# Gram, R and attention value products over the whole TensorE array: keys and queries beside zeros, values stored twice

## The chip, the core and the metric

The kernel runs on one core of a Trainium2 chip. TensorE (PE) multiplies, VectorE (DVE), ScalarE (ACT) and GpSimd (POOL) do the elementwise work, and nearly all transfers are issued from SyncE's queue (SP). The metric is the device time in microseconds (us); less is better. Three runs of the kernel before took 4266.24, 4277.43 and 4285.46 us; the median is 4277.43 us.

## The reference

Two layers of an encoder are applied to a sequence of 2048 tokens and one of 512, with 1024 channels, in float32. Layer 0 is a pair of gated linear recurrences. Layer 1 (where the change lies) is window attention and RWKV-7 time mixing side by side, then an output product, residual and layer norm. What matters of layer 1:

```python
def banded_window_attention(q, k, v, sink):     # 8 heads of 64, 2 groups of keys and values, 128 keys either way
    s = jnp.einsum('bnigrd,bnjgd->bngrij', qb, kb).astype(jnp.float32) * (hd ** -0.5)
    ...
    p = jnp.exp(s - lse[..., None])
    o = jnp.einsum('bngrij,bnjgd->bnigrd', p.astype(vb.dtype), vb)

def rwkv7_scan(r, log_w, k, v, kk, a):          # 8 heads of 64, both directions
    def step(S, inp):
        r_t, w_t, k_t, v_t, kk_t, b_t = inp
        s_kk = jnp.einsum('bhvk,bhk->bhv', S, kk_t)
        S = S * w_t[:, :, None, :] - s_kk[..., None] * b_t[:, :, None, :] + v_t[..., None] * k_t[:, :, None, :]
        return S, jnp.einsum('bhvk,bhk->bhv', S, r_t)
```

## The kernel before

Tokens come in 5 blocks of 512. Layer 0 and the projections of both layers come first; the change lies behind them, in `layer1_core`, and in the two things that feed it: the scratch `z_scr` that `rwkv_dirs` writes, and `rwkv_post`.

`layer1_core` works on 20 steps (4 pairs of heads by 5 blocks), each in two directions and two halves of 4 chunks of 64 tokens: 80 halves. For a half, `stageA` loads `Z` (the tile `Zc`: scaled keys and queries of two heads, one on partitions 0 to 63, the other on 64 to 127) and makes on TensorE: the **Gram products** (`gram`, 2 heads by 4 chunks, each over the 64 partitions of its head); the transposed keys (`bk`, 4 transpositions); the **R products** (`rps`, per chunk one product for each head with 64 columns of weights from `LR`, and with the head's tile `SW` of 128 columns as the moving operand, where 64 rows of `SW` are an identity and 64 are values). `inverse` inverts 16 by 16 triangles on DVE, `stageT` widens the inverses with many small products (`px`, `py`, 32 by 32), multiplies them with R (`t`), overwrites the identity rows of `SW` with the result, makes `fin`, and then writes the identity back into `SW` for the next half that uses it (`unit_rows`, on POOL). `chain` carries the state from chunk to chunk: a product, two DVE additions, a transposition, an ACT copy.

`attend` is the window attention, 40 tiles of 128 queries: four heads' `score` products, the softmax on DVE and ACT, then per head the transposed probabilities (`pt<-pr`) and the **value products** (`po<-pT,vw`, 64 columns of weights, 128 moving columns, up to 3 key tiles). It holds one of two PSUM tiles of its pool for `po` during all four heads.

A lane of generators for each of these is advanced in turn; the build's scheduler then orders the instructions of each engine by its own estimates, with `stageT`, `chain` and `inverse` given priority. The engines take their instructions in that order. `rwkv_post` (head norm and gate of a block) runs for the first block beside the end of the core, in four buffers of its own; the output product `out_proj` follows it.

A product of float32 operands shows as two MATMUL records with a weight load (LDWEIGHTS) each: 640 Gram products are 1280 records. In a row, `64*128` is the part of the array that the weights take (rows and columns), and the shape behind it is the moving operand.

Of the kernel before, what the change touches and what calls it, by code (L numbers as in the profile page):

```python
# [10 lines left out]
F32 = mybir.dt.float32  # L11
# [10 lines left out]
NB = 512  # L22
# [18 lines left out]
class Common:  # L41
# [86 lines left out]
    def split(self, x, hi, lo, eng=None):  # L128
        """x into two float32r parts"""
# [4 lines left out]
    def mm2(self, out, lhsT, x):  # L134
        """product of a matrix that float32r holds exactly with two parts"""
# [7 lines left out]
    def ln_exp(self):  # L143
        """the table set of ScalarE that has both the logarithm and the exponential"""
        self.tc.keep_in_program_order(self.nc.scalar.preload_act_table_set("natural_log_exp_and_others"))

# [16 lines left out]
    # ---- products of column tiles with a block of tokens; a block comes in parts of some k-tiles, and the parts  # L163
    # stream through the buffers (one more than the parts) of one tag: [128, k-tiles, (hi, lo), tokens] ----
    def stream(self, order, load, parts):
        """order: the blocks in turn; load(i, f): part f of entry i"""
# [16 lines left out]
    def projs(self, ws, last=False):  # L183
        """one or two column tiles, part by part; last: the last of this block"""
# [17 lines left out]
    def mod_init(self):  # L202
# [9 lines left out]
        # sums the rows 32 j + s of each sequence s  # L212
# [7 lines left out]
    def mod_tiles(self, l, w, t0, nt):  # L220
        """nt column tiles of the modulation product from loaded weights w [128, 8, nt * 128]: the conditioning
        vectors stand in four column groups, each summing two of the k-tiles; the groups are added in the transposition"""
# [21 lines left out]
    def mod_first(self):  # L244
        """shift and scale of layer 0"""
# [10 lines left out]
    def mod_rest(self):  # L256
        """gate of layer 0 and all of layer 1, beside the projections"""
# [12 lines left out]
    def gate_rows(self, l, pool):  # L270
        """1 + gate over the free axis, the same on every partition"""
# [96 lines left out]
class Even(Common):  # L368
# [9 lines left out]
    def even_layer(self, mk_emit):  # L378
# [4 lines left out]
        with ExitStack() as ctx:  # L383
# [6 lines left out]
            self.wk = self.pool(ctx, "wk")  # L390
            self.sm = self.pool(ctx, "sm", 2)
# [19 lines left out]
    def even_consts(self):  # L411
# [11 lines left out]
        # lower bounds: softmax over the two logits, first entry  # L423
# [7 lines left out]
        # f = lb + oml * sigmoid(z) = (lb + oml / 2) + oml / 2 * tanh(z / 2); the halves of q and 1 - f go with nol  # L431
# [8 lines left out]
        # low-rank gate weights of GLA, stacked [hi; hi; lo]  # L440
# [36 lines left out]
    def seq_sums(self, s, n):  # L477
        """sums over the chunks of a sequence, with room for a shift by one either way: the sums of chunk c stand at
        c + 2 (forward) or c (backward), and the states before it at c + 1, where those of the chunk it follows stood"""
# [5 lines left out]
    def decay(self, lf, rows, rev, b, bc, cols, nch0):  # L485
        """rows: partitions. b: running sums in each chunk, bc: the same less its middle; cols: middle, end less middle."""
# [15 lines left out]
    def silu_from(self, ps, out, tag="sg"):  # L502
        """twice the SiLU: (1 + tanh(x / 2)) x"""
# [4 lines left out]
    def att(self, kf, qf, kb, qb):  # L508
        """masked chunk products of both directions, summed: [128 j, 4, 128 i]"""
# [35 lines left out]
    def post(self, o, col, b):  # L545
        """head RMS norm, gate, and the two float32r parts to scratch"""
# [21 lines left out]
    def out_split(self, y, col, b, pool=None):  # L568
        nc = self.nc
        yh, yl = (pool.tile([128, NB], F32R, tag=x, bufs=1 + (pool is not self.wk), name=x) if pool else self.wt(x, dt=F32R) for x in ("yh", "yl"))  # L570
# [1177 lines left out]
```

## Time and profile before

| | us |
|---|---|
| median of three runs | 4277.43 |
| span of the profiled execution | 4263.0 |
| PE busy in the span | 3864.8 (91%) |
| DVE, ACT, POOL busy | 2844.7, 2178.4, 1257.9 |
| stretch of `stageA`, 2640 to 3806 us: PE busy | 1131.58 of 1166 |
| the same stretch: DVE, ACT, POOL busy | 817.79, 680.03, 323.64 |

The profiled execution's own time is its span and some 14 us around it, taking the median of the runs for it (4277.43 - 4263.0). A matmul is busy in the record from its start to its last result, and matmuls overlap, so PE's busy share is near 100% wherever it always has work; what a group costs PE is read from the starts of the groups around it in the timeline. The granted clock (PEclk) is 1.00 where TensorE has its 2.4 GHz, and 0.50 where it has 1.2 GHz.

### The profile page before, as it was taken

The page shows a single profiled execution, that of the slowest core. Times are in us where ns is not written, and L with a number is a line of the kernel's source. Part 1 is how long each engine was busy: PE and PEld are TensorE (multiplying, and loading weights), DVE is VectorE, ACT ScalarE, POOL GpSimd, SP SyncE. Part 2 cuts the span into 40 slices and gives each one's busy share as a digit, 9 for nine tenths or more (in the row PEclk, how much of TensorE's full clock was granted, in tenths as well). Part 3 has the DMA queues.
Part 4 walks back from the last instruction along what each step waited for, and adds up shares of the span by engine and source line. Part 5 has one row for each costly group of instructions (what it writes and reads, how often), then busy time and mean ns, then how long its engine had stood idle before and what let it go on. Part 6 is the DMA issues. An engine that isn't in the chain of part 4 may idle for free.

```text
span 4263.0 us, 76423 instructions
## 1 busy us (share of the span) xinstructions
PE 3864.8 (91%) x28536; PEld 3097.3 (73%) x28536; DVE 2844.7 (67%) x6350; ACT 2178.4 (51%) x4214; POOL 1257.9 (30%) x1561
## 2 busy tenths in 40 slices
PE   6999999998888699998999897999999999997688
PEld 4878787767676478776878676778778777775467
DVE  4554545466766589577666767677767766775798
ACT  4565757455455522345544546555556555564220
POOL 1020212112211254324232422223223222233784
PEclk8999999999999799999999998989989998996799
DMA  7544544456555477678687777344344433433675
GB/s 270 198 158 149 198 163 147 175 202 214 196 210 196 144 244 244 222 255 266 230 286 242 243 248 216 102 109 107 104 104 116 104 103 97 109 98 112 217 235 179
DMA packets 672115, 768.58 MB, mean 180 GB/s; under 512 B 243680, under 2 KB 538464, under 8 KB 646144
## 3 DMA queue, kind: packets, MB, share of 16 engines
q1 hardware_dynamic: 671744, 763.69, 55.4%
q8 instruction: 226, 3.70, 0.4%
q14 instruction: 145, 1.19, 0.1%
HBM read 533.84 MB, written 220.20 MB: 177 GB/s over the span
## 4 chain that ended last, share of the span: by engine, by line
PE 31%; DVE 11%; DMA 6%; ACT 3%; issue 2%; POOL 2%; SPq 1%; POOLq 0%; DVEq 0%; ACTq 0%
PE pp L126 10%; PE gram L126 3%; PE po L126 3%; PE rps L126 2%; PE fin L126 2%; PE chain L126 2%; PE pt L141 2%; PE t L126 2%; PE py L126 1%; PE px L126 1%; PE chain L141 1%; PE score L126 1%; DVE tmp L116 1%; PE bk L141 1%; DVE Z L116 1%
## 5 line engine op out<-in xcount | busy, mean ns | idle before, releaser
L126 PE MATMUL pp<-h,whi 128*128 128x512 f32 (+2 forms) x4800 | 1560.1, 403 | 83.7 <-DMA h<-h_scr 25.4
L126 PEld LDWEIGHTS pp<-h,whi 128*128 128x128 f32 (+2 forms) x4800 | 892.1, 190 | 294.5 <-DMA h<-h_scr 25.6
L126 PE MATMUL pp<-h,wlo 128*128 128x512 f32 (+2 forms) x2400 | 955.4, 399 | 5.0 <-POOL wlo L113 5.0
L126 PEld LDWEIGHTS pp<-h,wlo 128*128 128x128 f32 (+2 forms) x2400 | 454.3, 189 | 110.0 <-POOL wlo L113 7.5
L110 ACT ACT_TABLE_LOAD x227 | 291.2, 1283 | 23.1 <-DVE cl L499 10.4
L126 PE MATMUL pp<-owh,oh 128*128 128x512 f32 x640 | 258.6, 405 | 18.8 <-DMA oh<-o_scr 16.7
L126 PE MATMUL pp<-owh,ol 128*128 128x512 f32 x640 | 255.9, 401 | 15.6 <-DMA ol<-o_scr 15.6
L126 PE MATMUL pp<-owl,oh 128*128 128x512 f32 x640 | 258.2, 404 | 0.0
L113 POOL TENSOR_TENSOR wlo<-wst,whi 128x512 fp32r<-128x512 f32 (+3 forms) x87 | 162.1, 1869 | 246.7 <-ACT whi L110 244.2
L1312 POOL COPY LD<-GS 32x128 f32<-32x128 f32 x320 | 116.9, 365 | 355.5 <-ACT GS L1309 346.8
L113 POOL TENSOR_TENSOR at<-abuf,abuf 64x256 f32<-64x256 f32 x80 | 63.7, 796 | 518.7 <-DVE abuf L529 449.2
L126 PE MATMUL gram<-Zc 64*128 64x128 f32 x1280 | 202.6, 300 | 8.8 <-DMA Zc<-z_scr 7.1
L113 DVE TENSOR_TENSOR SS<-chain,OH 64x64 f32<-64x64 f32 x608 | 135.1, 222 | 109.7 <-PE chain L126 98.7
L113 POOL TENSOR_TENSOR tmp<-tmp 128x512 fp32r<-128x512 f32 x80 | 118.5, 1481 | 254.7 <-ACT tmp L110 208.4
L126 PEld LDWEIGHTS gram<-Zc 64*128 64x128 f32 x1280 | 160.9, 196 | 42.2 <-issue 18.5
L1257 POOL COPY SW<-c_ident 64x512 f32<-64x512 f32 x160 | 106.7, 668 | 271.6 <-PE fin L126 231.5
L126 PE MATMUL fin<-GB,SW 128*128 128x128 f32 x1280 | 176.4, 280 | 2.1 <-ACT OH L1424 1.9
L110 ACT ACTIVATE S<-chain,ecol 128x128 f32<-128x128 f32 x320 | 116.3, 368 | 113.5 <-PE chain L141 110.3
L113 POOL TENSOR_TENSOR ptmp<-ptmp 128x512 f32<-128x512 f32 (+1 forms) x100 | 146.0, 1473 | 84.4 <-ACT ptmp L110 39.5
L126 PEld LDWEIGHTS fin<-GB,SW 128*128 128x128 f32 x1280 | 158.6, 193 | 10.6 <-ACT OH L1424 3.6
L126 PEld LDWEIGHTS pp<-owh,oh 128*128 128x128 f32 x640 | 124.9, 195 | 48.5 <-DMA oh<-o_scr 15.0
L126 PE MATMUL chain<-RX,S 128*128 128x128 f32 x608 | 145.5, 327 | 13.6 <-DVE od L113 10.1
(324 smaller groups left out, 8418.4 us busy)
## 6 DMA issues: line engine op xcount, KB each, us to landing
h<-h_scr SPq DMA_DIRECT2D x70, 2048.0 KB, 9.4
h<-h_scr SPq DMA_DIRECT2D x80, 1024.0 KB, 7.5
z_scr<-Z SPq DMA_DIRECT2D x40, 1024.0 KB, 4.6
Zc<-z_scr SPq DMA_DIRECT2D x80, 512.0 KB, 4.0
h_scr<-h SPq DMA_DIRECT2D x10, 2048.0 KB, 7.7
oh<-o_scr SPq DMA_DIRECT2D x40, 512.0 KB, 5.7
ol<-o_scr SPq DMA_DIRECT2D x40, 512.0 KB, 6.6
h_scr<-h1s SPq DMA_DIRECT2D x20, 1024.0 KB, 5.3
```

The lines of the kernel that those rows point to most:

```text
L110: self.nc.scalar.activation(out=out, in_=in_, func=func, bias=bias, scale=scale)
L113: (eng or self.nc.vector).tensor_tensor(out=out, in0=a, in1=b, op=op)
L116: (eng or self.nc.vector).scalar_tensor_tensor(out=out, in0=a, scalar=s, in1=b, op0=op0, op1=op1)
L126: self.nc.tensor.matmul(out=out, lhsT=lhsT, rhs=rhs, start=start, stop=stop)
L141: self.nc.tensor.transpose(out, in_, self.ident[0:n, 0:n])
L1257: nc.gpsimd.tensor_copy(sw[h][Q[h]], self.ident[Q[h]].unsqueeze(1).to_broadcast([64, 4, 128]))
L1312: nc.gpsimd.tensor_copy(LD[blk, cs], gs[blk, :, 32 * i:32 * i + 32])
```

## The change

- **Gram:** `Z` keeps only the weights' half. The moving half is loaded into one of two fixed tiles `KR`, zeroed once, where each head's columns stand beside zeros in the other head's partitions. A product takes all 128 partitions.
- **R:** the two products per chunk are now one of `kr` (128 columns of weights, both heads) with a 64-column identity `II`, and one of `la` (128 columns, both heads, a single fixed tile with zeros off the diagonal) with `vs`, the values of both heads, loaded a second time. Each has 64 moving columns instead of 128. `SW` needs no identity rows any more: `unit_rows` (two POOL copies per half) and 16 ACT copies ahead of the core go; the second copy of `t` into `SW` swaps its halves.
- **Attention:** values are loaded twice side by side, so that the weights have 128 columns; the probabilities of four heads are transposed into one tile, and one product per key tile has 512 moving columns. Half of its result is used; the gate product is two DVE instructions instead of one.
- `z_scr` has another layout. `rwkv_post` beside the core takes its buffers from the pool of the attention, under the tag that the probabilities use (5 buffers for both). Comments are dropped.

```diff
@@ rwkv_consts, rwkv_dirs @@
-        self.z_scr = self.dram.tile([4, 2, nb, 128, 8, 256], F32, name="z_scr")
+        self.z_scr = self.dram.tile([4, 2, nb, 128, 2, 8, 128], F32, name="z_scr")
...
-            Z = self.wk.tile([128, 8, 256], F32, tag="Z", bufs=1, name="Z")
+            Z = self.wk.tile([128, 2, 8, 128], F32, tag="Z", bufs=1, name="Z")
@@ layer1_core @@
-            def unit_rows(sw):
-                for h in range(2):
-                    nc.gpsimd.tensor_copy(sw[h][Q[h]], self.ident[Q[h]].unsqueeze(1).to_broadcast([64, 4, 128]))
             for i in range(NS):
                 for d in range(2):
                     for h in range(2):
-                        o = Q[1 - h]
-                        (nc.vector, nc.gpsimd)[h].memset(SW[d][i][h][o, :, Q[h]], 0.0)
-                        nc.scalar.copy(SW[d][i][h][Q[h]], self.ident[Q[h]].unsqueeze(1).to_broadcast([64, 4, 128]))
+                        (nc.vector, nc.gpsimd)[h].memset(SW[d][i][h][Q[1 - h], :, Q[h]], 0.0)
+
+            KR = [zeroed(f"KR{i}", [128, 4, 2, 2, 64], nc.gpsimd) for i in range(2)]
+            la = zeroed("LA", [128, 4, 128], nc.vector)
+            II = cp.tile([128, 64], F32, name="II")
+            for h in range(2):
+                nc.vector.tensor_copy(II[Q[h]], self.ident[Q[h], Q[h]])
+            nA = [0]
...
-                        Z = lp.tile([128, 4, 256], F32, tag="Z", bufs=2, name="Zc")
-                        nc.sync.dma_start(out=Z, in_=self.z_scr[p, d, b, :, cs])
-                        nc.sync.dma_start(out=rho, in_=self.z_scr[p, d, b, :, cs, 64:128])
-                        LR = lp.tile([128, 4, 128], F32, tag="LR", bufs=2, name="LR")
+                        kr = KR[nA[0] % 2]
+                        nA[0] += 1
+                        Z = lp.tile([128, 4, 128], F32, tag="Z", bufs=2, name="Zc")
+                        nc.sync.dma_start(out=Z, in_=self.z_scr[p, d, b, :, 1, cs])
+                        for hd in range(2):
+                            nc.sync.dma_start(out=kr[Q[hd], :, :, hd],
+                                              in_=self.z_scr[p, d, b, Q[hd], 0, cs].rearrange("p c (a t) -> p c a t", t=64))
+                        nc.sync.dma_start(out=rho, in_=self.z_scr[p, d, b, :, 0, cs, 64:128])
+                        vs = lp.tile([128, 4, 64], F32, tag="vs", bufs=2, name="vs")
                         for hd in range(2):
                             o = Q[1 - hd]
-                            nc.sync.dma_start(out=LR[Q[hd], :, Q[hd]], in_=self.z_scr[p, d, b, Q[hd], cs, 0:64])
+                            nc.sync.dma_start(out=vs[o], in_=self.v_scr[p, d, b, :, cs, o])
                             nc.sync.dma_start(out=sw[hd][o, :, o], in_=self.v_scr[p, d, b, :, cs, o])
...
-                                self.mm(ps[:, c], Z[q, c, 128:256], Z[q, c, 0:128])
+                                self.mm(ps[:, c].rearrange("p (a t) -> p a t", t=64), Z[:, c], kr[:, c, :, hd])
...
-                            self.tt(LR[o, :, q], gs[o, :, 0:64], mS[o], ALU.mult)
+                            self.tt(la[o, :, q], gs[o, :, 0:64], mS[o], ALU.mult)
...
-                        rp = pr.tile([128, 4, 128], F32, tag="t", name="rps")
+
+                        rp = pr.tile([128, 4, 2, 64], F32, tag="t", name="rps")
                         for c in range(4):
-                            for hd in range(2):
-                                self.mm(rp[Q[hd], c], LR[:, c, Q[hd]], sw[hd][:, c])
-                        nc.scalar.copy(R, rp)
+                            self.mm(rp[:, c, 0], kr[:, c, 0].rearrange("p h t -> p (h t)"), II)
+                            self.mm(rp[:, c, 1], la[:, c], vs[:, c])
+                        nc.scalar.copy(R, rp.rearrange("p c a t -> p c (a t)"))
...
-                            unit_rows(sw)
...
-                        self.add("post", self.rwkv_post(i, nb_, self.wk, 4))
+                        self.add("post", self.rwkv_post(i, nb_, self.ap, 5))
@@ attend @@
-        V = ap.tile([128, 6, 64], F32, tag="vw", bufs=1, name="vw")
-        nc.sync.dma_start(out=V[:, 0:(w1 - w0) // 128], in_=self.av_scr[g, :, w0 // 128:w1 // 128])
+
+        V = ap.tile([128, 6, 128], F32, tag="vw", bufs=1, name="vw")
+        for i in range(2):
+            nc.sync.dma_start(out=V[:, 0:(w1 - w0) // 128, 64 * i:64 * i + 64],
+                              in_=self.av_scr[g, :, w0 // 128:w1 // 128])
...
-                for i in range(nt):
-                    self.mm(po[r, hd // 2], V[:, (k0 - w0) // 128 + i], pT[:, i * 128:(i + 1) * 128],
-                            start=(i == 0), stop=(i == nt - 1))
+            po = self.pa.tile([128, 2, 2, 128], F32, tag="s", name="po")
+            for i in range(nt):
+                self.mm(po.rearrange("p a b q -> p (a b q)"), V[:, (k0 - w0) // 128 + i],
+                        pT[:, i].rearrange("p h q -> p (h q)"), start=(i == 0), stop=(i == nt - 1))
```

PE's order in the middle of the core, before (`chain`, `px`, `rps`, `gram`, `po`, `pt` as above):

```order
L126 MATMUL po<-pT,vw 64x128 x3
L141 MATMUL pt<-c_ident,pr 128x128 x3
L126 MATMUL rps<-SW_21670,LR 64x128
L126 MATMUL gram<-Zc 128x128 x4
L126 MATMUL chain<-RX,S_30413 128x2x64
L126 MATMUL px<-TT,LO 32x32 x5
L126 MATMUL chain<-RX,S_30456 128x2x64
L126 MATMUL px<-TT,LO 32x32 x4
L126 MATMUL po<-pT,vw 64x128 x3
L141 MATMUL pt<-c_ident,pr 128x128 x3
```

And about as far on, after:

```order
L126 MATMUL rps<-vs,LA 128x64
L126 MATMUL chain<-RX,S_29766 128x2x64
L126 MATMUL gram<-KR_21700,Zc 128x128 x2
L126 MATMUL chain<-RX,S_29779 128x2x64
L126 MATMUL gram<-KR_21700,Zc 128x128
L126 MATMUL t_29577<-R,TL_21656 128x128
```

Of the ten groups before, each takes another part of the array than the one ahead of it; of the six after, all take the whole array, and only `px` and `py` take less.

SP's order in the same part of the core, after (`lm` and `acc_scr` belong to the inverses and the states, `q`, `gt`, `yh`, `yl` to the attention):

```order
L1300 DMA Zc<-z_scr 128x512
L1302 DMA KR_21700<-z_scr 64x8x64
L1648 DMA o_scr<-yh 128x2x128
L1602 DMA gt<-ag_scr 128x2x128
L1648 DMA o_scr<-yl 128x2x128
L1302 DMA KR_21700<-z_scr 64x8x64
L1308 DMA vs<-v_scr 64x4x64 x2
```

A half now has eight loads where it had six, and a load of `KR` waits for the R products of two halves earlier, as one of `LR` did.

The end of the core on PE, before (`dg` makes the gate rows of `out_proj`, `cmean` and `bmean` are the products of `rwkv_post`, `pp` are those of `out_proj`):

```order
L126 MATMUL pt<-ptmp,cmean 128x512
L141 MATMUL chain<-c_ident,SS_21662 128x128
L141 MATMUL chain<-c_ident,SS_21666 128x128
L126 MATMUL pt<-dg,allones 128x128 x2
L126 MATMUL pt<-ptmp,bmean 128x512
L126 MATMUL pt<-dg,allones 128x128 x2
L126 MATMUL pt<-ptmp,bmean 128x512
L126 MATMUL pt<-dg,allones 128x128 x12
L126 MATMUL pp<-owh_39959,oh 128x512
```

And after:

```order
L141 MATMUL chain<-c_ident,SS_21666 128x128
L126 MATMUL pt<-ptmp,bmean 128x512
L126 MATMUL pt<-dg,allones 128x128 x4
L126 MATMUL pt<-ptmp,bmean 128x512
L126 MATMUL pt<-dg,allones 128x128 x12
L126 MATMUL pt<-ptmp,cmean 128x512 x2
L126 MATMUL pt<-ptmp,bmean 128x512 x2
L126 MATMUL pp<-owh_39546,oh 128x512
```

Before, half of the fourth head's `rwkv_post` stands behind the last state; after, half of the third and all of the fourth.

## Rows read from the trace of the kernel before

**Rows 1.** The page's first line.

```profile
span 4263.0 us, 76423 instructions
```

**Rows 2.** Windows: length, busy time (instructions) by engine, PEclk, DMA share, GB/s.

```profile
2640.00:3806.00 1166.00, 1131.58 (x14238) 914.62 (x14237) 817.79 (x2953) 680.03 (x1666) 323.64 (x738) 0.93 0.41 107
3806.00:3942.00 136.00, 99.68 (x858) 77.36 (x856) 89.73 (x268) 71.66 (x159) 50.26 (x49) 0.73 0.35 108
```

**Rows 3.** PE's longest wait, 2640 to 3806: us in total, times, longest.

```profile
PE chain L141 <- DVE SS L113: 10.6, 19, 1.1
```

**Rows 4.** Groups on PE, 2640 to 3806: count | busy, mean ns | idle before.

```profile
L126 PE MATMUL po<-pT,vw 128*64 128x128 f32 x815 | 131.6, 296 | 1.2 <-ACT pT L1623 1.2
L126 PE MATMUL rps<-SW,LR 128*64 128x128 f32 x1280 | 130.7, 296 | 1.4 <-DMA SW<-v_scr 1.1 <-ACT GS L1309 0.2
```

**Rows 5.** Timeline of PE: start, us, then the group; here neighbours differ in shape.

```profile
3216.84 1.16 PE L126 MATMUL gram<-Zc 64*128 64x128 f32 x8
3217.93 0.49 PE L126 MATMUL chain<-RX,S 128*128 128x128 f32 x2
3218.34 0.31 PE L126 MATMUL px<-TT,LO 32*32 32x32 f32 x10
3218.58 0.49 PE L126 MATMUL chain<-RX,S 128*128 128x128 f32 x2
3219.00 0.26 PE L126 MATMUL px<-TT,LO 32*32 32x32 f32 x8
3219.19 0.87 PE L126 MATMUL po<-pT,vw 128*64 128x128 f32 x6
3219.99 0.55 PE L141 MATMUL pt<-c_ident,pr 128*128 128x128 f32 x3
```

**Rows 6.** The same view where neighbours have the whole array; the last row does not.

```profile
3206.08 0.60 PE L141 MATMUL bk<-c_ident,Zc 128*128 128x128 f32 x4
3206.52 0.39 PE L126 MATMUL chain<-RX,S 128*128 128x128 f32 x2
3206.74 1.06 PE L126 MATMUL t<-R,TL 128*128 128x128 f32 x8
3207.63 0.27 PE L141 MATMUL chain<-c_ident,SS 128*128 128x128 f32 x1
3207.84 1.09 PE L126 MATMUL rps<-SW,LR 128*64 128x128 f32 x14
3208.85 0.38 PE L126 MATMUL fin<-GB,SW 128*128 128x128 f32 x1
```

**Rows 7.** Weight loads of 128 columns ahead of two moving columns, timeline of PEld.

```profile
38.55 0.41 PEld L126 LDWEIGHTS pt<-c_msel,modrow 98*128 98x128 f32 x3 [4.51 <-ACT modrow L235]
30.43 1.78 PEld L126 LDWEIGHTS pt<-c_msel,modrow 98*128 98x128 f32 x8 [7.55 <-ACT modrow L235]
```

**Rows 8.** Windows either side of a fall of the granted clock.

```profile
3162.00:3169.00 7.00, 6.92 (x182) 5.34 (x177) 5.27 (x21) 4.00 (x13) 1.56 (x4) 1.00 0.62 172
3169.00:3192.00 23.00, 23.00 (x181) 17.62 (x181) 11.92 (x51) 5.88 (x17) 2.45 (x6) 0.50 0.14 39
```

**Rows 9.** SP's longest wait, 2640 to 3806: us in total, times, longest.

```profile
SPq L1301 <- PE rps L126: 64.7, 32, 5.5
```

**Rows 10.** DMA issues, 2640 to 3806: KB each, median us to landing.

```profile
Zc<-z_scr SPq DMA_DIRECT2D x78, 512.0 KB, 4.0
LR<-z_scr SPq DMA_DIRECT2D x156, 64.0 KB, 2.5
```

**Rows 11.** ACT at the start of the core.

```profile
2627.72 10.02 ACT L1263 COPY SW<-c_ident 64x512 f32<-64x512 f32 x16
```

**Rows 12.** PE at the start and at the end of the core.

```profile
2634.85 3.09 PE L126 MATMUL gram<-Zc 64*128 64x128 f32 x16 [5.50 <-DMA Zc<-z_scr]
3914.97 0.82 PE L141 MATMUL chain<-c_ident,SS 128*128 128x128 f32 x2
3942.16 0.80 PE L126 MATMUL pp<-owh,oh 128*128 128x512 f32 x1 [12.31 <-DMA oh<-o_scr]
```

More of the change, by code (lines that the diff above doesn't have):

```diff
@@ L390, in even_layer @@
             self.wk = self.pool(ctx, "wk")
+            self.ap = None
             self.sm = self.pool(ctx, "sm", 2)
@@ L569, in out_split @@
         nc = self.nc
-        yh, yl = (pool.tile([128, NB], F32R, tag=x, bufs=1 + (pool is not self.wk), name=x) if pool else self.wt(x, dt=F32R) for x in ("yh", "yl"))
+        yh, yl = (pool.tile([128, NB], F32R, tag=x, bufs=1 + (pool is not self.ap), name=x) if pool else self.wt(x, dt=F32R) for x in ("yh", "yl"))
         self.act(yh, y, AF.Copy)
@@ L1201, in rwkv_dirs @@
             nc.vector.tensor_copy(self.ecol[:, p, d, db * 8:db * 8 + 8], e1[:, :, 64])
-            Z = self.wk.tile([128, 8, 256], F32, tag="Z", bufs=1, name="Z")
-            self.tt(Z[:, :, 0:64], view(kk), e1[:, :, 0:64], ALU.mult)
-            self.tt(Z[:, :, 64:128], view(r), e1[:, :, 1:65], ALU.mult, nc.gpsimd)
-            self.stt(Z[:, :, 128:192], view(X1), self.xsc[:, 0:1], e2, ALU.mult, ALU.mult)
-            self.stt(Z[:, :, 192:256], view(X2), self.xsc[:, 1:2], e2, ALU.mult, ALU.mult)
+            Z = self.wk.tile([128, 2, 8, 128], F32, tag="Z", bufs=1, name="Z")
+            self.tt(Z[:, 0, :, 0:64], view(kk), e1[:, :, 0:64], ALU.mult)
+            self.tt(Z[:, 0, :, 64:128], view(r), e1[:, :, 1:65], ALU.mult, nc.gpsimd)
+            self.stt(Z[:, 1, :, 0:64], view(X1), self.xsc[:, 0:1], e2, ALU.mult, ALU.mult)
+            self.stt(Z[:, 1, :, 64:128], view(X2), self.xsc[:, 1:2], e2, ALU.mult, ALU.mult)
             nc.sync.dma_start(out=self.z_scr[p, d, db], in_=Z)
@@ L1317, in stageA @@
                         for c in range(4):
-                            self.tr(bk[:, c], Z[:, c, 128:256])
+                            self.tr(bk[:, c], Z[:, c])
                         for hd in range(2):
@@ L1411, in stageT @@
                     nc.scalar.copy(sw[0][Q[0]], t1[Q[0]])
-                    nc.scalar.copy(sw[1][Q[1]], t1[Q[1]])
+                    nc.scalar.copy(sw[1][Q[1]].rearrange("p c (a t) -> p c a t", t=64)[:, :, ::-1],
+                                   t1[Q[1]].rearrange("p c (a t) -> p c a t", t=64))
                     yield
@@ L1599, in attend @@
                     self.mm(ps[:, 0:nk], q[:, hd], K[:, i, k0 - w0:k1 - w0], start=(i == 0), stop=(i == 1))
-                pr = ap.tile([128, 384], F32, tag="pr", bufs=5, name="pr")
+                pr = ap.tile([128, 384], F32, tag="ptmp", bufs=5, name="pr")
                 h = 4 * g + hd
@@ L1614, in attend @@
             nc.vector.reciprocal(out=rd, in_=den)
-            po = self.pa.tile([128, 2, 128], F32, tag="s", name="po")
+            pT = ap.tile([128, 3, 4, 128], F32, tag="pT", bufs=1, name="pT")
             for hd in range(4):
@@ L1621, in attend @@
                     self.tr(pt[:, i * 128:(i + 1) * 128], pr[:, i * 128:(i + 1) * 128])
-                pT = ap.tile([128, 384], F32, tag="pT", name="pT")
-                nc.scalar.copy(pT[:, 0:nk], pt[:, 0:nk])
+                nc.scalar.copy(pT[:, 0:nt, hd], pt[:, 0:nk].rearrange("p (i q) -> p i q", q=128))
                 yield
-                r = slice(64 * (hd % 2), 64 * (hd % 2) + 64)
-                for i in range(nt):
-                    self.mm(po[r, hd // 2], V[:, (k0 - w0) // 128 + i], pT[:, i * 128:(i + 1) * 128],
-                            start=(i == 0), stop=(i == nt - 1))
+            po = self.pa.tile([128, 2, 2, 128], F32, tag="s", name="po")
+            for i in range(nt):
+                self.mm(po.rearrange("p a b q -> p (a b q)"), V[:, (k0 - w0) // 128 + i],
+                        pT[:, i].rearrange("p h q -> p (h q)"), start=(i == 0), stop=(i == nt - 1))
             y = ap.tile([128, 2, 128], F32, tag="yo", bufs=1, name="yo")
-            self.tt(y, po, gt, ALU.mult)
+            for i in range(2):
+                r = slice(64 * i, 64 * i + 64)
+                self.tt(y[r], po[r, :, i], gt[r], ALU.mult)
             yh = ap.tile([128, 2, 128], F32R, tag="yh", bufs=1, name="yh")
```

## The prediction

> **What bounds the kernel now.** I read the windows first. In the stretch where `stageA` runs, 2640 to 3806 us, PE is busy for 1131.58 of 1166 us, and DVE, the next, for 817.79 [rows 2]. The waits then say whether "busy" means "bound": PE's longest wait in the stretch adds up to 10.6 us [rows 3], and the R and the value products wait 1.4 and 1.2 us in over 2000 records [rows 4]. So PE nearly always has an instruction ready, and what an instruction holds of PE is what it costs. That is read from the timeline, start to start, not from the mean duration (296 ns for a record of which PE starts the next far sooner).
>
> Two pieces of the timeline are to be laid side by side. Where neighbours all use the whole array, a `chain` product of two records takes 3206.74 - 3206.52 = 0.22 us and eight records of `t` take 3207.63 - 3206.74 = 0.89 us, 0.11 us each [rows 6]. Where each neighbour uses another part of the array, the same `chain` product takes 0.41 and 0.42 us, eight Gram records of the same streaming length take 1.09 us, and six value records 3219.99 - 3219.19 = 0.80 us, where six at 0.109 would be 0.65 [rows 5]. So a group that is cut off on both sides by a change of shape costs 0.15 to 0.20 us more. Each group has one change at its start, so this is the price of one change of shape. PE's order from the first Gram product to the last R product has 1558 such changes before; at 0.16 us they are 249 us of the 1166.
>
> **The change part by part.** Everything is summed against the profiled execution, span 4263.0 us [rows 1], with 14.4 us between that and the median (4277.43 - 4263.0).
>
> *Changes of shape.* With Gram, R and value products on the whole array only `px` and `py` are narrow. Counted in the same part of PE's order there are 518 changes after, so 1040 go. I take 0.16 us, near the lower end of 0.15 to 0.20 [rows 5, 6], because most of the removed groups are value and R products with 64 columns of weights: -166 us (-156 to -208).
>
> *Gram.* Same number of records, and 128 moving columns in both. In the narrow form a record costs (1.09 - 0.20)/8 = 0.11 us, in a full one 0.11 [rows 5, 6]: 0.
> A rule that speaks against the change: the Trainium skill, TensorE: Matmul & The Clock Gate, section "Part 3: Packing small matmuls — row/col tiling", says that products of fewer than 128 rows placed in different row groups run at once, so that filling the array with zeros throws half of it away. By that rule the two heads' Gram products would have run side by side and the sum would be 80 x 16 x 0.055 = 70 us worse. The rows do not bear it out for this kernel: the eight records of one head follow each other in one row group at full price, and the other head's come later.
>
> *R products.* Here the array was really shared: fourteen records alternate between the two column halves and take 3208.85 - 3207.84 = 1.01 us, change of shape included [rows 6]; less some 0.2 for that, 0.055 to 0.06 us each. Afterwards there are again sixteen records per half, each with 64 moving columns, half of 0.11. But each loads 128 columns of weights. No row of before has that form; the nearest have 128 columns of weights and only two moving columns: three loads take 0.41 us at the full clock, eight take 1.78 at half, in starts 0.11 and 0.21 us apart (a load itself showing as 0.19 and 0.33) [rows 7]. So the weight load, not the streaming, sets 0.11 us. Per half 16 x (0.112 - 0.055) = 0.91, by 80 halves: +73 us. The other end is 0: weights wholly hidden, 0.055 as before. I take the upper end, since that row differs only in moving columns.
>
> *Value products.* Per tile of queries, 24 records at 0.109 were 2.6 us; now 6 records of four times the columns, 4 x 0.109 = 0.44 each, are 2.6: 0. Their changes of shape are counted above. `po` no longer holds a PSUM tile during the transpositions, which can only help; the gate product in two DVE parts adds some 0.4 us forty times on an engine that is not the bound: 0.
>
> *Clock.* The granted clock averages 0.93 in the stretch [rows 2], so it is at half for 14% of it, 163 us, worth 82 us of PE at the full clock. It falls although PE is never idle: in 3162 to 3169 PE is busy for 6.92 of 7 us with small `py` products, R and Gram products, and the 23 us after that are at half [rows 8]. Full-array products in the place of narrow ones should make such falls rarer; the `px` and `py` stretches stay. I take -25 us (0 to -60).
>
> *Loads, POOL, ACT.* Two more issues per half on SP, and none of SP's queue is the bound; the loads of `KR` wait for R products two halves back, as those of `LR` did (64.7 us in total, 5.5 at most [rows 9]), and behind them in the queue stand `vs`, `SW` and `rho` of later halves. A half takes 1166/80 = 14.6 us and a 512 KB load lands in 4.0 us [rows 10]: hidden, 0. What it costs uncovered is a rival below. The 160 copies of `unit_rows` leave POOL, which has time (323.64 of 1166): 0.
>
> *Start.* Sixteen identity copies hold ACT for 10.02 us [rows 11], and the first evacuation stands behind them; the first Gram product waits for its load 5.50 us and starts at 2634.85 [rows 12]. Two POOL memsets and the loads of `KR` take the place of the copies: -4 us (-8 to 0).
>
> *End.* From the last state (3914.97) to the first output product (3942.16) there are 27 us [rows 12], in which the fourth head's `rwkv_post` ends. Now a head and a half stand there. Against that, the attention ends earlier and the last steps have fewer changes of shape. I set 0, with -20 to +25.
>
> *Sum.* PE loses 166 - 73 + 25 = 118 us of the stretch. Not all comes out as time: DVE would go from 70% of the stretch (817.79 of 1166) to 79% (some 832 of 1048), and waits of PE for DVE and ACT that are covered today will show. I take four fifths, -94. With the start, -98: span 4165, and 4165 + 14.4 = **4179 us**.
>
> **The rivals.**
> - *More than that.* If the weight load is hidden after all, PE loses 166 + 25 = 191 us and four fifths are 153; if the clock stays up (-60) and nothing else shows, PE loses 153 whole. Either way 4277.4 - 153 - 4 = 4120. For it: PE's waits are tiny. Against: the weight load row.
> - *Waits take the freed time.* The `chain` of states goes PE, DVE, PE, ACT, and PE's largest wait today is of this kind [rows 3]; the order was made by a scheduler's estimates, not by these costs. If two thirds of the 118 us return as waits, and the start is kept: 4277.4 - 39 - 4 = 4234; with the worse end, 4259. For it: DVE at 79% with bursts. Against: 10.6 us is little to begin with.
> - *Slower: the loads of `KR` show.* A Gram product now needs two loads that may start only when the R products of two halves back are done; the queue behind them waits too. If in half of the 80 halves PE stands for one landing and two issues, 4.0 + 0.6 us [rows 10], that is +184: 4277.4 + 184 - 98 = 4363. It decides from the point where R products and the next Gram product on the same `KR` lie under 5 us apart; evenly spread they are a half apart, 14.6 us, so only a bunched order does it.
>
> **How the numbers follow.** Chances: the forecast 0.60 (its own range 4130 to 4230), more than that 0.15, waits 0.16, slower 0.09. The range runs from 4100 (below the 4120 of the first rival, some of it left out) to 4250 (most of the second); the third and the worst of the second stay outside. A measurement of this kernel tells about 0.5% from no change, 21 us: faster means under 4256, slower over 4299. The first two cases and about 0.09 of the third give faster 0.84; the rest of the waits gives same 0.07; `KR` gives slower 0.09.
>
> **What would show it.** Right: in PE's timeline a `chain` product between Gram groups takes 0.22 us; R records start 0.11 us apart; the stretch of `stageA` is some 90 us shorter, with PE still busy nearly throughout; PEclk above 0.93. Wrong: R records at 0.06 (first rival); PE's waits for DVE of several tens of us (second); Gram products waiting for `KR` (third); a longer way from the last state to the output product than 27 us plus 25; Gram records on the full array dearer than 0.11.

## The result, and the profile of the changed kernel

The changed kernel takes 4168.09 us (median; 4163.97 to 4174.11) against 4275.95 of the kernel before on the same chip: ratio 0.975, 95% interval 0.9726 to 0.9774. The forecast was 4179, with a range of 4100 to 4250. The profiled execution is 96.8 us shorter than that of [rows 1].

The page's first line, and the windows of the stretch of `stageA` and of what lies between it and the first output product (length, busy time by engine, PEclk, DMA share, GB/s), to be laid beside [rows 1, 2]:

```profile
span 4166.2 us, 75101 instructions
...
2640.00:3712.00 1072.00, 1009.45 (x13582) 889.96 (x13582) 816.12 (x3008) 664.24 (x1676) 226.82 (x593) 0.96 0.49 118
3712.00:3850.00 138.00, 91.73 (x846) 67.03 (x845) 83.05 (x254) 69.76 (x149) 42.85 (x35) 0.75 0.38 121
```

The stretch is some 94 us shorter, PE is still busy for 94% of it (97% before), and the granted clock is 0.96 instead of 0.93. DVE has the same 816 us to do in less time, 76% of it.

PE's waits and groups in the same stretch, which answer to [rows 3, 4], and SP's longest wait, for [rows 9]:

```profile
PE chain L141 <- DVE SS L113: 16.0, 24, 1.9
PE rps L126 <- DVE LA L113: 5.6, 7, 1.5
PE gram L126 <- DMA KR<-z_scr: 2.5, 2, 2.2
...
L126 PE MATMUL gram<-KR,Zc 128*128 128x128 f32 x1280 | 188.5, 287 | 5.5 <-DMA KR<-z_scr 2.5 <-DMA vs<-v_scr 1.5 <-ACT R L1334 0.6
L126 PE MATMUL rps<-vs,LA 128*128 128x64 f32 x640 | 124.8, 278 | 5.9 <-DVE LA L113 5.6
L126 PE MATMUL rps<-II,KR 128*128 128x64 f32 x640 | 123.3, 276 | 2.6 <-ACT GS L1316 2.5
L126 PE MATMUL po<-pT,vw 128*128 128x512 f32 x204 | 98.6, 614 | 0.0
...
SPq L1302 <- PE rps L126: 60.5, 20, 9.4
```

The loads of `KR` do wait in SP's queue for R products, as those of `LR` did, but Gram products wait for them for 2.5 us in all. The rival in which they show had needed 184.

The timeline of PE (start, us, group) for R products and for a piece in which every neighbour uses the whole array, as in [rows 6]:

```profile
3066.56 0.39 PE L126 MATMUL rps<-II,KR 128*128 128x64 f32 x2
3066.78 0.39 PE L126 MATMUL rps<-vs,LA 128*128 128x64 f32 x2
3067.01 0.39 PE L126 MATMUL rps<-II,KR 128*128 128x64 f32 x2
...
3072.48 0.39 PE L126 MATMUL chain<-RX,S 128*128 128x128 f32 x2
3072.70 1.50 PE L126 MATMUL t<-R,TL 128*128 128x128 f32 x12
3074.04 1.06 PE L126 MATMUL gram<-KR,Zc 128*128 128x128 f32 x8
3074.93 0.27 PE L141 MATMUL chain<-c_ident,SS 128*128 128x128 f32 x1
```

Starts, not durations: two R records take 3066.78 - 3066.56 = 0.22 us, eight Gram records 3074.93 - 3074.04 = 0.89, a `chain` product 3072.70 - 3072.48 = 0.22. That is 0.11 us a record for all three, and the 0.15 to 0.20 us that a change of shape cost in [rows 5] are gone here.

PE at the start and at the end, for [rows 12]:

```profile
2644.71 3.55 PE L126 MATMUL gram<-KR,Zc 128*128 128x128 f32 x16 [2.19 <-DMA KR<-z_scr]
...
3805.09 0.98 PE L141 MATMUL chain<-c_ident,SS 128*128 128x128 f32 x2 [0.24 <-DVE SS L113]
...
3850.17 0.80 PE L126 MATMUL pp<-owh,oh 128*128 128x512 f32 x1 [18.72 <-DMA oh<-o_scr]
```

**Where PE's time went.** For each PE record between the first Gram and the last R product I took from the trace the time from its start to the start of the next, and put it into four accounts. *Own steps*: what a record takes among neighbours of its shape at the full clock. *Changes*: what the last step ahead of a change of shape and the first one behind it take beyond that, at the full clock. *Half clock*: what all steps at half clock take beyond their own steps, the changes of shape that fall there included. *Idle*: gaps of PE over 20 ns. In us:

| | before | after | difference | predicted |
|---|---|---|---|---|
| own steps | 821 | 894 | +73 | +73 |
| changes of shape (number) | 222 (1558) | 69 (518) | -153 | -166 |
| half clock (time at it) | 91 (163) | 44 (86) | -47 | -25 |
| idle | 36 | 60 | +24 | +24 |
| first Gram to last R | 1170 | 1067 | -103 | -94 |

Of the 1558 changes before, 141 fell in half clock, and 41 of the 518 after, so part of the third row belongs to the second. At the full-clock price (222/1417 = 0.157 us before, 69/477 = 0.145 after) these are 22 and 6 us. Put with the changes, they make the differences -169 and -31, beside -166 and -25 predicted.

The first Gram product starts 10 us later, and from the last R to the end it is 3 us shorter: -103 + 10 - 3 = -96, the difference of the spans.

### The profile page after: what moved, and what is told of

Same layout as the page of the kernel before. It is cut to its first block, busy times and chain, and to the rows that moved or that the text cites. A ratio compares the mean times of both kernels' runs of the same rounds, so it can differ in the third digit from the quotient of the medians.

```text
span 4166.2 us, 75101 instructions
## 1 busy us (share of the span) xinstructions
PE 3743.6 (90%) x27864; PEld 3067.3 (74%) x27864; DVE 2838.6 (68%) x6393; ACT 2149.8 (52%) x4198; POOL 1145.3 (27%) x1403
## 5 line engine op out<-in xcount | busy, mean ns | idle before, releaser
L126 PE MATMUL gram<-KR,Zc 128*128 128x128 f32 x1280 | 188.5, 287 | 5.5 <-DMA KR<-z_scr 2.5
L126 PEld LDWEIGHTS gram<-KR,Zc 128*128 128x128 f32 x1280 | 170.6, 201 | 8.6 <-ACT R L1334 3.1
L126 PEld LDWEIGHTS pp<-owh,ol 128*128 128x128 f32 x640 | 124.7, 195 | 37.7 <-DMA ol<-o_scr 11.7
L126 PE MATMUL chain<-RX,S 128*128 128x128 f32 x608 | 134.6, 310 | 14.0 <-DVE od L113 7.8
```

The costliest lines, as they stand in the source:

```text
L126: self.nc.tensor.matmul(out=out, lhsT=lhsT, rhs=rhs, start=start, stop=stop)
```

## The experiments

The same accounts for all kernels below, each from one profiled execution; the ratio is to the kernel before on the same chip, with its interval. In brackets behind the changes stand their number and how many of them fell in half clock.

| kernel | ratio | own steps | changes (number, in half clock) | half clock (time at it) | idle | first Gram to last R |
|---|---|---|---|---|---|---|
| after, again | 0.9772 (0.9744 to 0.9800) | 894 | 70 (518, 38) | 40 (79) | 61 | 1065 |
| a_gram_narrow | 0.9982 (0.9965 to 1.0) | 875 | 125 (977, 196) | 151 (271) | 46 | 1197 |
| a_gram_alt | 0.9872 (0.9851 to 0.9893) | 874 | 128 (918, 95) | 91 (172) | 41 | 1134 |
| after_without_r | 0.9751 (0.9729 to 0.9774) | 850 | 122 (830, 11) | 21 (42) | 81 | 1074 |
| after_r_32 | 0.9788 (0.9756 to 0.9821) | 904 | 64 (526, 77) | 78 (153) | 63 | 1108 |
| before_buffers | 1.0010 (0.9986 to 1.0035) | 825 | 216 (1541, 144) | 80 (142) | 34 | 1156 |
| before_gram | 0.9840 (0.9806 to 0.9875) | 832 | 155 (1105, 69) | 40 (72) | 59 | 1086 |
| before_val_buffers | 0.9941 (0.9915 to 0.9966) | 835 | 168 (1140, 90) | 72 (132) | 61 | 1137 |
| before_r_buffers | 1.0082 (1.0052 to 1.0112) | 871 | 175 (1335, 190) | 128 (232) | 24 | 1198 |
| after_r_transposed | 0.9686 (0.9669 to 0.9704) | 867 | 70 (496, 16) | 29 (58) | 75 | 1041 |
| after_val_halves | 0.9647 (0.9621 to 0.9672) | 862 | 95 (680, 36) | 45 (89) | 61 | 1063 |
| halves_best | 0.9593 (0.9576 to 0.9611) | 832 | 94 (643, 10) | 15 (31) | 58 | 999 |

Of the clock, one profiled execution says little. The mean granted clock of the whole execution is on record for every run: 0.929 to 0.940 in 42 runs of the kernel before beside these kernels, 0.939 to 0.944 in the eight of the changed kernel, 0.923 to 0.929 in the ten of a_gram_narrow, 0.933 to 0.936 in the four of a_gram_alt, 0.941 to 0.949 in the four of before_gram, 0.926 to 0.931 in the four of before_r_buffers. For before_buffers (0.928 to 0.943), before_val_buffers (0.930 to 0.936) and after_r_32 (0.935 to 0.944) it overlaps that of the kernel they are compared with.

**The array shape of Gram alone.**

```
- self.mm(ps[:, c]..., Z[:, c], kr[:, c, :, hd])
+ self.mm(ps[:, c]..., Z[q, c], kr[q, c, :, hd])
```

> The changed kernel, but each Gram product reads only the 64 rows of its head (weights and moving data cut to that half, same loads, same zeros in memory, same results). The only thing undone is the array shape of the Gram products: 977 changes of shape from the first Gram to the last R product against 518 in the changed kernel. My theory (a change of shape costs 0.16 us, a Gram record 0.11 us in either form, four fifths come out as time): +459 x 0.16 = +73 us of PE, +59 to +73 us of time, so 4227 to 4241 against 4168. Rival, the gain came from elsewhere (fewer instructions, POOL and ACT relieved, another order): 4168, within 10 us. Rival, filling the array with zeros threw away half of it: faster than 4168.

Measured 4265.18 us: one slice takes back nearly the whole gain, over 20 us more than my theory allowed. The accounts say why. The changes cost 125 - 69 = 56 us more at the full clock, and PE stands at half clock for 271 us instead of 86, which costs another 107. Some 25 of these 107 are changes of shape that fell in half clock (196 instead of 41, at 0.16). So the 459 changes cost some 80 us, near the 73 expected, and the clock, which the theory left out, some 80 more. The window from the first to the last R product:

```profile
2649.00:3841.00 1192.00, 1146.17 (x13641) 962.96 (x13640) 813.77 (x3004) 679.05 (x1677) 231.65 (x587) 0.89 0.44 105
```

The same window of the changed kernel, executed again (`after_again`):

```profile
2653.00:3713.00 1060.00, 998.97 (x13552) 880.07 (x13550) 808.86 (x2987) 660.09 (x1663) 226.68 (x588) 0.96 0.49 118
```

> The changed kernel once more, beside the three above on the same chip: 4168, within 8 us. What it is for is the time at half clock in the stretch: 86 us in the first profile; if it is 60 to 110 again, a difference of 80 us between kernels is theirs and not chance; if it moves by 80 us between two executions of one kernel, nothing is to be read from such a difference.

Measured 4171.98, and 79 us at half clock after 86: the time of this kernel moved little between two executions, and a difference of 185 us is the other kernel's. The granted clocks of all runs, 0.923 to 0.929 against 0.939 to 0.944, say the same.

**Two heads alternating on the two row halves.**

```
+ for c in range(4):
+     for hd in range(2):
+         self.mm(gram[hd][:, c]..., Z[Q[hd], c], kr[Q[hd], c, :, hd])
```

> The changed kernel with Gram products on 64 rows as in a_gram_narrow, and the two heads' products alternating record by record into two PSUM tiles, so that the two row halves of the array could work at once. 918 changes of shape. My theory, 64-row float32 products don't overlap: Gram records stay 0.11 us apart, +400 x 0.16 = +64, 51 to 64 us of time, 4219 to 4232. Rival, two row halves do run at once when they alternate: 0.055 us per record, 80 x 16 x 0.055 = 70 us less, four fifths 56, so 4163 to 4176.

Measured 4219.95, as expected without overlap. But the order that the scheduler made does not do what the edit asks for. In 59 of the 80 halves the four products of one head still stand ahead of the four of the other, as in the kernel before and in a_gram_narrow; 10 halves alternate throughout and 11 in part. The timeline of PE has both kinds, at the full clock, first eight records of one head, then sixteen of two heads that alternate:

```profile
2984.04 1.16 PE L126 MATMUL gram<-KR,Zc 64*128 64x128 f32 x8
2985.13 0.49 PE L126 MATMUL chain<-RX,S 128*128 128x128 f32 x2
...
3121.91 1.16 PE L126 MATMUL gram<-KR,Zc 64*128 64x128 f32 x16
3123.01 0.33 PE L141 MATMUL chain<-c_ident,SS 128*128 128x128 f32 x1
```

Eight records of one head take 1.09 us, sixteen alternating ones 1.10, each with its change of shape: (1.09 - 0.17)/8 = 0.115 us a record against (1.10 - 0.17)/16 = 0.058. Two row halves do run at once where the two heads alternate. The Trainium skill, TensorE: Matmul & The Clock Gate, section "Part 3: Packing small matmuls — row/col tiling", has products in different row groups run at once; the trace agrees. What the rival would be worth in time stays open, since most halves do not alternate: what the zeros cost against a kernel whose Gram products alternate all through was not measured.

The 45 us between this kernel and a_gram_narrow are hardly in the products: 60 of the 63 us between their stretches are in the account of half clock, of which some 16 are changes of shape that fell there (95 instead of 196). The products have the same form in both, but the scheduler's order of everything around them differs too, so what in the order moves the clock is not shown.

**R as before, the rest of the change kept** (128x64 products of both heads, identity rows in `SW`):

```
- self.mm(rp[:, c, 0], kr[:, c, 0]..., II)
- self.mm(rp[:, c, 1], la[:, c], vs[:, c])
+ self.mm(rp[Q[hd], c], LR[:, c, Q[hd]], sw[hd][:, c])
```

> The changed kernel with the R products as before: 128x64 products of the two heads side by side, identity rows kept in SW and refilled on POOL. 830 changes of shape against 518. My theory: +312 x 0.16 = +50 us for the changes, -73 us for the R records back at 0.055 us, together -23, four fifths -18: 4150 against 4168, so the R part of the change loses a little. Rival, the full weight load is hidden (records at 0.055 in the changed kernel too): +50, four fifths +40: 4208.

Measured 4167.19, neither: the same as the changed kernel. Its R steps are 44 us cheaper and 23 us of half clock are gone, but 312 changes of shape come back (+53) and PE idles 21 us more. The R part of the change is worth nothing beside the other two. That is a miss of both expectations: I had expected it to lose 18.

**What sets an R record** (both products of a chunk move 32 columns, and half of R is left out; the second product is shown):

```
- self.mm(rp[:, c, 1], la[:, c], vs[:, c])
+ self.mm(rp[:, 2 * c + 1], la[:, c], vs[:, c, 0:32])
```

> The changed kernel with R products that move 32 columns instead of 64; the other half of each R block is a copy of the first, so half of R is left out of the computation. 526 changes of shape against 518. My theory, the load of 128 weight columns sets the pace: R records stay 0.10 to 0.11 us apart: 4168, within 10 us. Rival, the streaming of 64 columns sets it: records at 0.05 to 0.06, 80 x 16 x 0.05 = -64 us of PE, four fifths -51: 4117.

Measured 4178.54, just outside the 10 us expected, and no gain from half the moving columns. PE's timeline:

```profile
3063.65 0.30 PE L126 MATMUL rps<-II,KR 128*128 128x32 f32 x2
3063.79 0.39 PE L126 MATMUL rps<-vs,LA 128*128 128x32 f32 x2
3064.01 0.39 PE L126 MATMUL rps<-II,KR 128*128 128x32 f32 x2
3064.24 0.39 PE L126 MATMUL rps<-vs,LA 128*128 128x32 f32 x2
3064.46 0.39 PE L126 MATMUL rps<-II,KR 128*128 128x32 f32 x2
```

Pairs start 0.22 us apart as with 64 columns. Only the first pair of the run is faster (0.14): there one step is 0.03 us. With 64 columns, in the changed kernel, the first pair takes 0.17 and that step 0.06:

```profile
2650.88 0.33 PE L126 MATMUL rps<-vs,LA 128*128 128x64 f32 x2
2651.05 0.39 PE L126 MATMUL rps<-II,KR 128*128 128x64 f32 x2
2651.27 0.39 PE L126 MATMUL rps<-vs,LA 128*128 128x64 f32 x2
```

So a record whose weights are already there takes a time that follows its moving columns, and one that has to load 128 columns of weights takes 0.11 us with 32 moving columns as with 64. The stretch is 41 us longer than the changed kernel's, most of it half clock (153 us for 86), but that is one execution, and over whole runs the two kernels' clocks overlap. The Trainium skill, TensorE: Matmul & The Clock Gate, section "LDWEIGHTS (loading the stationary operand)", puts a load at its columns divided by 1.2 in ns, whatever its depth: 107 ns for 128 by that formula. The 0.11 us agree.

**Each part by itself, on the kernel before.** The value part and the R part have no room on the chip by themselves: they would need 32.3 and 27.8 KB per partition where 30.7 and 26.4 are left. So all three parts get one side effect of the change, by which attention scores and `rwkv_post` share five buffers, and one kernel has nothing else.

```
- pr = ap.tile([128, 384], F32, tag="pr", bufs=5, name="pr")
+ pr = ap.tile([128, 384], F32, tag="ptmp", bufs=5, name="pr")
...
- self.add("post", self.rwkv_post(i, nb_, self.wk, 4))
+ self.add("post", self.rwkv_post(i, nb_, self.ap, 5))
```

> The kernel before with one side effect of the change alone: scores of the attention and rwkv_post share one set of five buffers. No product changes its form; 1541 changes of shape against 1558. My theory, the shared buffers are not what pays: within 10 us of before, 4275. If they lengthen the end, the way from the last state to the first output product is 45 us or more instead of 27, and the time up to 4295; if they also free the order of the attention, a gain of over 20 us in the stretch would say that part of the change's gain is theirs.

Measured 4277.15: no effect on the time. But from the last state to the first output product it is now 79 us:

```profile
3883.74 0.47 PE L141 MATMUL chain<-c_ident,SS 128*128 128x128 f32 x1 [0.28 <-DVE SS L113]
...
3962.83 0.77 PE L126 MATMUL pp<-owh,oh 128*128 128x512 f32 x1 [15.53 <-DMA oh<-o_scr]
```

It is 82 us in before_gram and before_r_buffers and 49 in before_val_buffers. The last state comes 31 us earlier, the product 21 us later: the shared buffers lengthen the end.

The three parts add to this the lines of the change shown above for Gram, R and values.

> The kernel before with the Gram part alone (keys and queries beside zeros, full-array Gram products; R and value products as before), and scores sharing rwkv_post's buffers as in the changed kernel, without which there is no room. 1105 changes of shape against 1558. At 0.155 us: -453 x 0.155 = -70 us of PE, four fifths -56: 4219 against 4275. Rival, narrow Gram products are what pulls the clock down (undoing them in the changed kernel brought 185 us more at half clock in the profile): another 40 to 60 us less of PE: 4160 to 4190, and under 80 us at half clock in the stretch where before has 158.

Measured 4206.54 (the kernel before 4267.09 here). Against before_buffers it has -61 us for changes and -40 at half clock; with those changes that fell in half clock (144 and 69) put to the changes, -73 and -28. A quarter of the sum came back as idle time (+25). So the clock, the rival's mechanism, is at work too (granted 0.941 to 0.949 in all four runs, 0.932 to 0.938 in the seven of the kernel before), but the time stays near my theory's. Gram alone takes 70 of the 89 us that before_buffers has over the changed kernel in the stretch.

> The kernel before with the value part alone and the shared buffers of before_buffers. 1140 changes of shape against 1541. At 0.155 us: -401 x 0.155 = -62 us of PE, four fifths -50 against before_buffers: about 4225. Rival, the clock is what pays: half clock as before (160 us), and then a gain only as large as the changes; with 100 us less at half clock another -40.

Measured 4236.92 (the kernel before 4267.93). Changes -48, half clock -8, own steps +10, idle +27: the stretch is only 19 us shorter, where 50 were expected. The shorter end (49 for 79) brings 30 more, so that the time comes near the 4225 expected is luck.

> The kernel before with the R part alone (zero-padded key tile and LA as full 128-column weights, 64 moving columns, stacked identity) and the shared buffers of before_buffers, without which there is no room; Gram and values as before. The scheduler orders it so that 1335 changes of shape stand there against 1541 of before_buffers. At 0.155 us: -206 x 0.155 = -32 us; R records from 0.055 to 0.10 or 0.11: +58 to +73; sum +26 to +41 of PE, four fifths +21 to +33: slower than before_buffers by that. Rival, the weight load costs nothing: -26. Rival, clock: narrow Gram products stay, so half clock stays at 160 us or more, which may move either by 30.

Measured 4303.51, 26 us slower than before_buffers, as expected, but not for the expected reason. Own steps +46, changes -41 and half clock +48; with the changes that fell in half clock (190 and 144) put to the changes, these are -34 and the clock +41. So my own terms make +12 (+46 - 34) where +26 to +41 were expected, and the rival's mechanism, the clock, makes the larger part.

**One R record fewer per chunk** (`vv` has the values beside zeros; to make room for it, one small tile of `inverse` goes, and the second copy of `t` no longer swaps its halves):

```
- self.mm(rp[:, c, 0], kr[:, c, 0]..., II)
- self.mm(rp[:, c, 1], la[:, c], vs[:, c])
+ nc.tensor.matmul(rp[:, c], kr[:, c, 0]..., self.ident, is_transpose=True, start=True, stop=False)
+ self.mm(rp[:, c], la[:, c], vv[:, c], start=False, stop=True)
```

> The changed kernel with R's key half made by one transposition of the zero-padded keys (one record of 128 columns) in place of a product with a stacked identity (two records of 64 columns), the value half added into the same PSUM tile from values beside zeros: 12 records per half of a block instead of 16, all on the full array, 496 changes of shape. My theory, every record with 128 columns of weights costs 0.11 us whatever it moves: 80 x 4 x 0.112 = -36 us, changes -22 x 0.16 = -3.5, four fifths of 39 are 32: 4136 against 4168. Rival, the streaming of 64 columns sets the R records (0.055) and those of 128 columns cost 0.11: 12 x 0.11 against 16 x 0.055, +35 us: 4203. Rival, R's time is not on the path: 4168.

Measured 4139.12, near the 4136 expected. Own steps fall by 27 us, half clock by 15, and 16 come back as idle time.

**Values on alternating column halves.**

```
- self.mm(po..., V[:, (k0 - w0) // 128 + i], pT[:, i]..., start=(i == 0), stop=(i == nt - 1))
+ for j in range(2):
+     self.mm(po[64 * j:64 * j + 64], V[:, (k0 - w0) // 128 + i], pT[:, i, j::2],
+             start=(i == 0), stop=(i == nt - 1))
```

> The changed kernel with only the value products changed as in halves_best (alternating column halves, values stored once). 680 changes of shape against 518. My theory: -52 + 162 x 0.15 = -28 us, four fifths -22: 4148 against 4170. Rival, no sharing: +24: 4190. Rival, the clock: up to +40 on top of the gain: 4150 to 4190.

> after_r_transposed, and the value products put back on halves of the array, but so that the halves alternate: values stored once, for each key tile one product of 256 columns (heads 0 and 2) on the left column half, then one (heads 1 and 3) on the right. 643 changes of shape against 496. My theory, alternating column halves share the array (the R products of before took 0.055 us a record of 128 columns): 12 records of 256 columns at some 0.11 instead of 6 of 512 at 0.43, 1.3 us less for each of 40 tiles, -52 us; +147 x 0.15 = +22 us; sum -30, four fifths -24: 4115 against 4139. Rival, column halves share nothing at this length: 0 + 22: 4157. Rival, the clock: narrow products bring more half clock, 0 to +40: 4139 to 4155.

Measured 4130.60 and, with the transposition, **4104.74**, 4.1% under the kernel before and better than the change. PE's timeline of halves_best:

```profile
3020.27 1.51 PE L126 MATMUL po<-pT,vw 128*64 128x256 f32 x10
3021.71 0.50 PE L126 MATMUL score<-kw,q 128*128 128x256 f32 x2
```

Ten records in 1.44 us with the change of shape: some 0.13 each for 256 columns, where the changed kernel takes 0.43 for one of 512, so 1.5 us a tile for 2.6. The two column halves share the array. The gain of the two kernels came in different places. In after_val_halves the stretch is hardly shorter (-4 us: own steps -32 of the -52 expected, changes +25); there the first Gram product starts 6 us earlier and the way to the output product is shorter by 18 us (last state 3797.95, output product 3824.42), and why has not been separated. That it gained more than the 22 us expected is therefore no proof of the sum behind them. In halves_best the stretch is 42 us shorter than in after_r_transposed: own steps -35, changes +24, half clock -14, idle -17.

## Why the prediction was right, step by step

*The bound.* PE, as read: 94% busy after, and PE's steps moved the time in nearly every experiment.

*Changes of shape, -166.* The count was exact (518 left), the price a little lower: 0.157 us before and 0.145 after, for those at the full clock. That is -153, and -169 with those that fell in half clock at the same price: near the forecast's number, for the forecast's reason. The Trainium skill, TensorEngine Tiling (Array Packing), section "Key Properties", says that changing the tiling mode drains TensorE; it gives no price; the 0.157 and 0.145 us are the trace's.

*Gram, 0, against the rule.* Mean step 0.107 us before, 0.112 after: +6. The prediction set the rule of the Trainium skill aside because the eight records of one head follow each other in the kernel before, and that reason held. The rule itself is borne out where two heads alternate (a_gram_alt, 0.058 us a record).

*R, +73.* The mechanism was right (after_r_32), the size too large: mean step 0.067 before, 0.105 after, 1279 x 0.038 = +49. Groups are cut up by other products, so before not all records had a partner in the other half, and after the first record of a group finds its weights loaded. That own steps come out at +73 all the same is luck: of the remaining +24, 6 are Gram's, some 10 lie in steps that end in a wait (81 at the full clock against 18 before), and the rest is not explained.

*Values, 0.* 816 x 0.109 = 89 us before, 204 x 0.43 = 88 after.

*Clock, -25.* Somewhat too small. The account has -47, but 16 of it are changes of shape that fell in half clock, and -31 are left. I had taken the falls as a small part of narrow products in general. a_gram_narrow shows that in the changed kernel Gram's shape moves the clock about as much as its changes of shape move the time directly (some 80 us each); in before_gram it is 28 against 73. What exactly brings a fall is open: in the changed kernel, too, the clock falls to half although PE is busy for 6.90 of the 7.50 us ahead:

```profile
3187.00:3194.50 7.50, 6.90 (x155) 5.13 (x154) 6.11 (x19) 3.78 (x11) 2.17 (x6) 1.00 0.60 132
3194.50:3208.00 13.50, 13.50 (x174) 12.16 (x175) 6.60 (x25) 6.13 (x18) 1.93 (x6) 0.50 0.43 110
```

Kernels with Gram products on 64 rows stand at half clock for 132 to 271 us, those on 128 rows for 31 to 153; the 153 are one execution of after_r_32, in which only the moving columns were cut; the others of that kind end at 89.

*Four fifths of it as time.* 24 us came back as idle time, one fifth of the 118 of the sum, and of the 127 measured (73 - 153 - 47). The fifth had been a guess, and that it came out is luck: in before_gram a quarter came back, in before_val_buffers 27 of 46.

*Loads, POOL, ACT, 0.* Right: 2.5 us of waits for `KR`.

*Start, -4.* Wrong in sign: the first Gram product starts 10 us later, the first R product at 2649.3 instead of 2642.0. I had looked at ACT's copies of the identity and not at SP's queue:

```profile
2639.48 1.90 SPq L1309 DMA_DIRECT2D SW<-v_scr  x3
2641.48 2.61 SPq L1302 DMA_DIRECT2D KR<-z_scr  x4
```

The first load of `KR` goes out behind those of `vs`, `rho` and `SW`, and the first Gram product waits for it.

*End, 0.* Right in sum, for two reasons that cancel. From the last R product to the last state 16 us less, from there to the output product 18 more (45 us). That the two cancel is luck. before_buffers shows that the shared buffers alone move the end in this way, and further (79 us).

*Sum.* The span came out at 4166.2, the sum had 4165: PE's steps lost 127 us instead of 118 (the clock 6 more, the changes 3 more), the idle time was as said, the start 14 the other way, the end 3 less. The small errors have both signs and nearly cancel; the largest term, the price of a change of shape, had been read from starts in a timeline and came out within 0.02 us. The 11 us between 4179 and 4168.09 are mostly the 14.4 us that I put between the profiled execution and the median. They are not time around the execution: in every run whose span is recorded, the time is 1.7 to 2.2 us longer than it. The execution profiled before was simply some 12 us faster than the median.

## What to carry to other kernels

Where PE is the bound, read its steps from start to start, count the changes of array shape in its order, and price one from two pieces of one timeline; here each float32 change cost 0.14 to 0.16 us, and 1040 of them were worth more than the own steps that the full-array forms added (169 us against 73). Whether two narrow products share the array has to be seen in their starts, and in the order that the scheduler really made: products on two column halves or two row halves did run at once where they alternated, and row halves cost the full price where one head's products stood together. A record that has to load 128 columns of weights costs 0.11 us here, with 32, 64 or 128 moving columns. An edit that alters what the array does from one record to the next can also alter the granted clock, so look at the time at half clock before a gain is put down to the edit's own arithmetic.

## What the runs showed of the hardware that I had not expected

- The time at half clock follows the form and the order of the products, with PE busy for 94 to 97% of the stretch: 271 us when only the slice of Gram's rows was cut, 172 when the same products stood in another order (a_gram_alt), 86 and 79 in two executions of the changed kernel.
- Fewer moving columns under full weights (after_r_32) gave nothing: 0.22 us a pair as before. Its 153 us at half clock, instead of 79 and 86, are one execution.
- Two row halves run at once where products alternate between them: sixteen float32 records of 64 rows in 1.10 us, where eight on one half take 1.09.
- A transposition and an ordinary product into the same PSUM tile, the second adding to the first, take 0.11 us a record like any other and saved one record in four.
- 256-column products on alternating column halves took some 0.13 us each.
